# Rotating 96 images by 180 degrees: the first load as two transfers of SyncE, 4 KB and 60 KB of each row, instead of 2 KB by ACT beside 62 KB by SyncE

## The chip, the cores and the metric

The kernel runs on one core of a Trainium2 chip. The metric is the device time of one execution in microseconds. Loads and stores are transfers between the chip's DRAM and the core's on-chip memory, which has 128 partitions. An instruction of SyncE (SP) or ScalarE (ACT) issues a transfer; the core's 16 DMA engines carry it out. Each of the two issuing engines has a queue of its own on all 16 DMA engines: q1 in the profile is SyncE's, q10 is ACT's. A packet here is one contiguous piece of one row.

## What is computed

The input x is float32 of shape 32 x 3 x 256 x 256, 25.17 MB. The output is each 256 x 256 image turned by 180 degrees:

```python
def reference(x):
    return np.rot90(x, k=2, axes=(-2, -1)).astype(np.float32)
```

A flat image of 65,536 elements turned by 180 degrees is the same list of elements in reverse order. There is no arithmetic; all bytes are read once and written once.

## The kernel before

The 96 images are cut into three groups of 32. In a group, each image lies over four partitions, a quarter (E = 16,384 elements, 64 KB) in each, so that a group fills a tile of 128 partitions by 64 KB. The three tiles A, Bt and Ct hold the whole input at once, and a small tile T of 128 x 2,048 is used for swapping.

To turn a group, two things happen. The function `inside` reverses the 16,384 elements of each partition in place, on VectorE: it takes a piece of 2,048 elements from the far end, reversed, into T, copies the matching piece of the near end, reversed, over the far end, and T over the near end. That is four rounds of three copies, 12 copies a tile, 36 in all, all on line 52. The first copy of a tile reads only its last 2,048 columns, and the second reads its first 2,048. The function `store` (line 58) then writes the tile out with the four quarters of each image in reverse order.

SyncE issues all transfers but one, in this order: the long part of A's load, Bt, Ct without its last 1,536 columns (`body`), the last 1,536 columns of Ct, a store of A's first 128 columns, the store of the rest of A, the store of Bt, the store of Ct. ACT issues one transfer, the first 512 columns (2 KB of each row) of A's load, line 70; it has no other work. All loads go through `load`, so that they appear under line 55 in the profile, and all stores under line 58.

An issuing engine waits, before a store, until what it stores has been written. SyncE issues in order, so a store that waits keeps all that follow it waiting. Line 79 adds one wait that the data don't need: the large store of A is not issued before `body` has landed. While SyncE waits for that, the DMA engines have the last 1,536 columns of Ct and the small store of A still to carry. Apart from that wait and VectorE's copies, which are kept in program order, the waits are worked out from which tile pieces an instruction reads and writes.

Of the kernel before, what the change touches and what calls it, by code (L numbers as in the profile page):

```python
# [2 lines left out]

os.environ.setdefault("NEURON_RT_ULTRASERVER_MODE", "4")

# [4 lines left out]

@with_exitstack
def kernel(
    ctx: ExitStack,
    tc: tile.TileContext,
    x: bass.AP,
    out: bass.AP,
):

    nc = tc.nc
    P = 128

    B, C, H, W = x.shape
    L = H * W
    G = 32
    E = L // 4
    J = E // 8

    x4 = x.rearrange("b c h w -> (b c) (h w)").rearrange(
        "(g n) (s e) -> g (n s) e", n=G, s=4)
    o4 = out.rearrange("b c h w -> (b c) (h w)").rearrange(
        "(g n) (s e) -> g n s e", n=G, s=4)  # L40

    pool = ctx.enter_context(tc.tile_pool(name="slots", bufs=1))
    A = pool.tile([P, E], x.dtype, tag="A")
    Bt = pool.tile([P, E], x.dtype, tag="B")
    Ct = pool.tile([P, E], x.dtype, tag="C")
    T = pool.tile([P, J], x.dtype, tag="T")

    def back(t, lo, hi):
        return t[:, hi - 1:(lo - 1 if lo else None):-1]

    def copy(dst, src):
        tc.keep_in_program_order(nc.vector.tensor_copy(out=dst, in_=src))  # L52

    def load(t, g, lo, hi, queue=nc.sync):
        return queue.dma_start(out=t[:, lo:hi], in_=x4[g][:, lo:hi])  # L55

    def store(t, g, lo, hi):
        return nc.sync.dma_start(
            out=o4[g][:, ::-1, lo:hi], in_=t[:, lo:hi])

    def inside(t):
        for lo in range(0, E // 2, J):
            hi = E - lo - J
            copy(T[:, :], back(t, hi, hi + J))
            copy(t[:, hi:hi + J], back(t, lo, lo + J))
            copy(t[:, lo:lo + J], T[:, :])

    TAIL = 1536
    HEAD = 512
    load(A, 0, 0, HEAD, nc.scalar)  # L70
    load(A, 0, HEAD, E)
    load(Bt, 1, 0, E)
    body = load(Ct, 2, 0, E - TAIL)
    load(Ct, 2, E - TAIL, E)
    inside(A)
    LEAD = 128
    store(A, 0, 0, LEAD)
    first = store(A, 0, LEAD, E)
    tc.add_manual_dep(
        first.ins, body.ins.name,  # L80
        mybir.DependencyInfo(mybir.DependencyClass.Sync, mybir.DependencyReason.DATA),
        reason="the first store is queued while the last strip is on its way")
    for g, t in ((1, Bt), (2, Ct)):
        inside(t)
        store(t, g, 0, E)

# [1 line left out]
_INS = ['x']  # L89
_OUTS = [((32, 3, 256, 256), 'float32')]  # L90

# [23 lines left out]
```

## Time and profile before

| | |
|---|---|
| median of 3 runs | 121.97 us (121.96 to 122.07) |
| the profiled execution | 121.97 us |
| its span in the trace | 120.2 us |
| VectorE busy | 44.2 us, 36 copies of 1.23 us |
| bytes moved | 25.17 MB read, 25.17 MB written |
| A's long load, issue to landing | 21.9 us |
| A's 2 KB load by ACT, issue to landing | 22.0 us |
| Bt's load, issue to landing | 40.8 us |
| Ct's store, issue to landing | 42.7 us |
| VectorE waits for A, Bt, Ct | 22.6, 4.3, 4.4 us |

The span runs from the first recorded instruction to the last; the rest of the 121.97 us lies around it. A time from issue to landing holds the time that a transfer waits in its queue behind others: Bt's load is issued at 1.18 us and lands when A's and Bt's bytes have both been carried.

### The profile page before, as it was taken

Reading aid. Unit: us, or ns where it says so; the run is one execution under the profiler, and the core shown is the slowest. Engines: PE = TensorE matmul, PEld = TensorE weight load, DVE = VectorE, ACT = ScalarE, POOL = GpSimd, SP = SyncE. Lnnn points to the kernel's source line nnn. Section 1 sums busy time; section 2 is a strip of 40 time slices with the busy share of each in tenths; the row PEclk is TensorE's granted clock in tenths of the full one; section 3 lists DMA queues with packets and bytes.
Section 4 is the critical chain, followed back from the end, with each engine's and each line's share of the span. In section 5 each row is a group of like instructions: output and inputs, shape, how many; then the busy total and the mean of one; then the engine's idle time right before and its main releaser. Section 6 shows DMA issues by size and latency. Waiting matters only on the chain.

```text
span 120.2 us, 97 instructions
## 1 busy us (share of the span) xinstructions
DVE 44.2 (37%) x36; POOL 0.2 (0%) x4
## 2 busy tenths in 40 slices
DVE  0000000499995099999059999500000000000000
POOL 0000000000000000000000000000000000000000
DMA  9888988899889879979499777988898889888990
GB/s 338 349 349 349 698 349 349 360 654 393 349 349 633 382 316 553 395 316 633 178 452 693 346 346 346 693 349 349 349 698 349 349 349 698 349 349 349 654 393 0
DMA packets 1296, 50.33 MB, mean 419 GB/s; under 512 B 144, under 2 KB 272, under 8 KB 528
## 3 DMA queue, kind: packets, MB, share of 16 engines
q1 hardware_dynamic: 1152, 50.07, 97.0%
q10 hardware_dynamic: 144, 0.26, 0.6%
HBM read 25.17 MB, written 25.17 MB: 419 GB/s over the span
## 4 chain that ended last, share of the span: by engine, by line
DMA 34%; DVE 25%; another core or an unknown queue 4%; issue 1%; SPq 0%; DVEq 0%
DMA Bt<-in_x_dram 34%; DVE T L52 8%; DVE Bt L52 8%; DVE Ct L52 8%; SPq L55 0%; DVEq L52 0%
## 5 line engine op out<-in xcount | busy, mean ns | idle before, releaser
L52 DVE COPY T<-A 128x2048 f32<-128x2048 f32 x4 | 4.9, 1226 | 22.7 <-DMA A<-in_x_dram 22.6
L52 DVE COPY T<-Ct 128x2048 f32<-128x2048 f32 x4 | 4.9, 1227 | 4.5 <-DMA Ct<-in_x_dram 4.4
L52 DVE COPY T<-Bt 128x2048 f32<-128x2048 f32 x4 | 4.9, 1226 | 4.4 <-DMA Bt<-in_x_dram 4.3
L52 DVE COPY Bt<-Bt 128x2048 f32<-128x2048 f32 x4 | 4.9, 1227 | 0.1
L52 DVE COPY A<-A 128x2048 f32<-128x2048 f32 x4 | 4.9, 1227 | 0.1
L52 DVE COPY A<-T 128x2048 f32<-128x2048 f32 x4 | 4.9, 1227 | 0.1
L52 DVE COPY Bt<-T 128x2048 f32<-128x2048 f32 x4 | 4.9, 1227 | 0.1
L52 DVE COPY Ct<-T 128x2048 f32<-128x2048 f32 x4 | 4.9, 1227 | 0.1
L52 DVE COPY Ct<-Ct 128x2048 f32<-128x2048 f32 x4 | 4.9, 1227 | 0.1
L100 POOL MEMSET const-bfloat16-1.0<- 128x1 bf16 x1 | 0.1, 101 | 0.0
L100 POOL MEMSET const-uint8-127<- 128x1 uint8 x1 | 0.1, 101 | 0.0
L100 POOL MEMSET const-float32-0.0<- 128x1 f32 x1 | 0.1, 98 | 0.2 <-issue 0.2
L100 POOL MEMSET const-float32-1.0<- 128x1 f32 x1 | 0.1, 98 | 0.0
## 6 DMA issues: line engine op xcount, KB each, us to landing
out_dram<-A SPq DMA_DIRECT2D x1, 8128.0 KB, 21.1
A<-in_x_dram SPq DMA_DIRECT2D x1, 7936.0 KB, 21.9
Ct<-in_x_dram SPq DMA_DIRECT2D x1, 7424.0 KB, 57.9
Ct<-in_x_dram SPq DMA_DIRECT2D x1, 768.0 KB, 59.3
A<-in_x_dram ACTq DMA_DIRECT2D x1, 256.0 KB, 22.0
out_dram<-A SPq DMA_DIRECT2D x1, 64.0 KB, 35.2
Bt<-in_x_dram SPq DMA_DIRECT2D x1, 40.8
out_dram<-Bt SPq DMA_DIRECT2D x1, 39.8
```

Source lines behind the costliest of these rows:

```text
L52: tc.keep_in_program_order(nc.vector.tensor_copy(out=dst, in_=src))
L100: nc = _bacc.Bacc("TRN2", target_bir_lowering=False, num_devices=1)
```

## The change

The function `load` loses its choice of queue; the first 1,024 columns of A (4 KB of each row) are now loaded by SyncE ahead of the other 15,360 (60 KB of each row), and ACT issues nothing.

```diff
-    def load(t, g, lo, hi, queue=nc.sync):
-        return queue.dma_start(out=t[:, lo:hi], in_=x4[g][:, lo:hi])
+    def load(t, g, lo, hi):
+        return nc.sync.dma_start(out=t[:, lo:hi], in_=x4[g][:, lo:hi])
...
     TAIL = 1536
-    HEAD = 512
-    load(A, 0, 0, HEAD, nc.scalar)
+    HEAD = 1024
+    load(A, 0, 0, HEAD)
     load(A, 0, HEAD, E)
     load(Bt, 1, 0, E)
     body = load(Ct, 2, 0, E - TAIL)
```

In the built program SyncE's list grows from eight transfers to nine, with the two parts of A first; the instructions of VectorE and GpSimd and their waits are the same.

## The prediction

> **What bounds the kernel now.** I read the page first, then the issue rows, then the waits of the DMA queue's own engine, then a table of stretches. The page:
>
> ```profile
> span 120.2 us, 97 instructions
> DVE 44.2 (37%) x36; POOL 0.2 (0%) x4
> ...
> DMA packets 1296, 50.33 MB, mean 419 GB/s; under 512 B 144, under 2 KB 272, under 8 KB 528
> ## 3 DMA queue, kind: packets, MB, share of 16 engines
> q1 hardware_dynamic: 1152, 50.07, 97.0%
> q10 hardware_dynamic: 144, 0.26, 0.6%
> ```
>
> VectorE works 37% of the span; the 16 DMA engines hold packets for 97.0 + 0.6 = 97.6% of it. q1 is SyncE's queue, q10 is ACT's; 144 packets on q10 are 128 rows of 2 KB and 16 four-byte completion writes. The page's chain of waits gives "DMA Bt" 34% and VectorE 25%, but it follows semaphores, and the store queue hides behind it. The waits of SyncE's queue show the real end:
>
> ```profile
> SPq L111 <- DMA out_dram<-Ct: 38.6, 1, 38.6
> SPq L58 <- DMA Ct<-in_x_dram: 33.1, 2, 32.5
> SPq L58 <- DMA A<-in_x_dram: 20.1, 1, 20.1
> SPq L58 <- DVE Ct L52: 15.2, 1, 15.2
> ```
>
> The last thing awaited is the last store, for 38.6 us, although VectorE was through at 76.7 us. So the time is: start of the transfer stream, plus the stream without a hole, plus the close.
>
> **The stream in numbers.** The packet records of the trace give one size, one duration: 512 B 27 ns, 2,048 B 84 ns, 6,144 B 234 ns, 59,392 B 2,192 ns, 63,488 B 2,342 ns, 65,024 B 2,399 ns, 65,536 B 2,418 ns. Each DMA engine carries 8 rows of every transfer, so one engine's work is 8 x (84 + 2,342 + 2,418 + 2,192 + 234 + 27 + 2,399 + 2 x 2,418) = 8 x 14,532 ns = 116.26 us. The start of the span:
>
> ```profile
> 0.73 0.38 ACTq L55 DMA_DIRECT2D A<-in_x_dram  x1
> 0.73 0.39 SPq L55 DMA_DIRECT2D A<-in_x_dram  x1
> 1.18 0.42 SPq L55 DMA_DIRECT2D Bt<-in_x_dram  x1
> 1.63 1.01 SPq L55 DMA_DIRECT2D Ct<-in_x_dram  x2
> ```
> ```profile
> 0.00:1.00 1.00, 0.00 (x0) 0.20 (x4) 1.00 0.00 0
> 1.00:2.00 1.00, 0.00 (x0) 0.00 (x0) 1.00 2.70 889
> 2.00:3.00 1.00, 0.00 (x0) 0.00 (x0) 1.00 0.34 127
> 3.00:4.00 1.00, 0.00 (x0) 0.00 (x0) 1.00 0.00 0
> 4.00:5.00 1.00, 0.00 (x0) 0.00 (x0) 1.00 1.22 528
> ```
>
> The first are start and duration of the issues. In the second the last two columns are DMA share and GB/s, booked to the stretch in which a packet starts: 889 GB/s in 1 us is 14 packets of 63,488 B, 127 is two more, and no further packet starts before 4 us. In the packet records the first of the 16 starts at 1.755 us, 1.02 us after the issue, fifteen by 2.08 and the sixteenth at 2.82. The fifteen take 2.89 to 3.30 us where later packets of the size take 2.34: an excess of 0.55 to 0.95 us, which I call the cold excess. All sixteen end at 4.78 to 5.22; less 2.342 that is as if data ran from 2.44 to 2.88 us on. ACT's packets, issued in the same instant as SyncE's, start only when the first long packet of their engine is over (4.78 us and on), and then the two queues alternate: a 2 KB row, a long row, a 2 KB row.
>
> Check of the sum: 2.88 + 116.26 = 119.14; the last data packet ends at 119.05. The last landing is at 119.39, and the span ends at 120.18. The profiled execution took 121.97 us, so 1.79 lies around the span, and it equals the median of the runs, 121.97; I work with its numbers as they are.
>
> **The change, part by part.**
>
> *ACT's issue goes.* One instruction of 0.38 us beside SyncE's of 0.39; ACT has no other work. Gain 0 on the path.
>
> *SyncE issues one more transfer, ahead of the others.* Its issues stand 0.45 us apart (0.73, 1.18, 1.63). So the 4 KB rows are issued at 0.73, the 60 KB rows at 1.18, Bt at 1.63 in place of 1.18, Ct's two from 2.08. Bt's packets are wanted when A's are through, at about 21.8 us, so 20 us hide the shift. Were there no such cover, 0.45 us would be paid.
>
> *The bytes.* Each engine has 8 packets of 4,096 B and 8 of 61,440 B for 8 of 2,048 and 8 of 63,488. Midway between the 2,048 B and 6,144 B rows is 159 ns, midway between 59,392 B and 63,488 B 2,267 ns. 8 x (159 + 2,267) = 19.41 us; before 8 x (84 + 2,342) = 19.41 us. Difference 0.
>
> *The hand-over from the first transfer to the second.* This is new: the engines now run dry unless the 60 KB packets are there when the 4 KB packets are through. The short ones last 8 x 0.159 = 1.27 us from when data runs, so to 2.44 + 1.27 = 3.71 us on the earliest engine. The second transfer, issued at 1.18, has packets at 1.18 + 1.02 = 2.20 if it goes as the first of them did, and 1.18 + 2.09 = 3.27 if as the latest. Margin 0.44 us at the worst. With no cold excess the short ones would be through at 1.755 + 1.27 = 3.03, and the latest engine would idle 0.24 us, which the vanished excess of 0.55 more than pays. So 0.
>
> *The cold excess with short packets* is in no row. Ends: it vanishes (-0.95 us, the largest excess), or it is paid again for the second transfer (+0.95); paid for each of 8 short packets (8 x 0.65 = +5 us) is excluded by the nearest rows: at 59 us the 6,144 B loads, also eight short packets in a row per engine at the same place of each row, keep 234 ns with one exception of 291, and 512 B stores keep 27 ns. These are warm, but they show that eight short reads in a row run without a gap. I take 0 change: the excess is once per engine at its first read, whatever the packet's length.
>
> *VectorE.* Its first copy reads the end of A's rows, so it waits for the long transfer alone (before: landed 22.59, ACT's part 22.76). In the new order the long rows are last on each engine, so it starts about 0.17 us later. Copies of A end at about 37.8 + 0.2; Bt lands at 41.96. Over 4 us hide it. The small store at 26.39 moves with it and is not wanted before 60.6 us.
>
> *The join of loads and stores.* The large store of A waits for Ct's long part (landed 59.56, issued 59.63, first packets 60.84) while 8 x (234 + 27) = 2.09 us of short packets cover it. Nothing of it changes but the engines' relative lag, now 0.44 us from first to last; the last engine has over 0.6 us of cover left (2.09 less landing and issue, 1.4 to 1.5), and it sets the end.
>
> Sum: 0, so **121.97 us**, give or take 0.2: half of the 0.44 us by which engines differ in their start, since the engine that ends last may be another.
>
> A rule that would make another sum. The two issues above stand side by side at 0.73, each as long as one alone (0.38 and 0.39, against 0.42 for Bt's). The Trainium skill (Perfetto Trace Analysis, "DMA Instruction — HWDGE (DVE, Sync)") says that the block which makes descriptors is shared by the two issuing engines and locked by one at a time, and counts the wait for the lock as part of the instruction; by it one of the two should last about 0.77 us, and if SyncE's descriptors stood behind ACT's, dropping ACT's would bring the stream forward by up to 0.38 us, to 121.59. The durations show no such wait, so the sum goes without it.
>
> **The rivals.**
>
> *Slower: the cold start is paid twice.* With long first packets, one read of 2.3 us covers everything that happens behind it. A short first transfer takes that cover away: if the 60 KB packets need not 2.09 but over 2.5 us from their issue at 1.18 (that is, are usable only after 3.7 us), the engines stand idle. From there it decides. For it: one of sixteen engines began 0.74 us after the other fifteen, and I see no transfer that starts behind an emptying queue at that point. Price: from nothing up to the excess once more, 0.95 us; the middle, with 0.55, gives 122.5; span of the case 122.2 to 122.9.
>
> *Faster: the cold excess comes from the two queues filling at once, or from sixteen long reads starting in step.* For it: the one engine that started late, at 2.82, took 2.349 us, no excess. Against it: that engine ended at 5.17, with the others, so it may only have been recorded late. Price: up to the whole excess, 121.0; likelier about half, 121.5; span 121.0 to 121.75.
>
> *The change does nothing that it says:* the program does have the two transfers first on SyncE and none on ACT, so this leaves only that all stays within the trace's scatter, which is the forecast.
>
> **How the numbers follow.** Forecast 0.57, slower rival 0.29, faster rival 0.14. A measurement of this kernel can tell about 0.2%, 0.24 us, from no change; the forecast's own range, 121.77 to 122.17, lies inside. The range for 8 in 10 takes the forecast whole, the slower rival up to 122.65 (about 0.2 of its 0.29) and the faster one down to 121.55 (about 0.06 of 0.14): 0.83. Faster 0.14, within 0.57, slower 0.29.
>
> **What would show it.** In the new trace: the first packet near 1.76 us; 4 KB packets of 159 ns after a first one with about 0.7 us more; the 60 KB packets starting from 3.7 to 4.2 us with no hole before them and 2,267 ns each, the first ones too. All packets of A end on the last engine near 22.15 us as before, VectorE starts at about 22.8. A hole between 4 KB and 60 KB packets, or long first 60 KB packets, is the slower rival; 60 KB packets from 3.1 to 3.5 us the faster one. I am wrong altogether if time is lost later than 5 us, for instance a hole at 60 to 62 us from a greater lag between engines.

## The result and the profile after

The changed kernel takes 122.41 us (median of 6 runs, 122.15 to 122.60) against 122.01 us (121.96 to 122.07) of the kernel before in the same comparison: ratio 1.003, 95% interval 1.0016 to 1.0043. It is slower, by about 0.4 us. Run again later beside other kernels it took 122.56 against 122.04, ratio 1.0038 (1.0025 to 1.0052). The profiled execution, 122.19 us, is one of the two quickest of its six, 0.22 us above the profiled one of before. A ratio here is the one that has an interval; it is not exactly the quotient of the two medians.

The page of the changed kernel, the lines that answer to those of before:

```profile
span 120.4 us, 97 instructions
...
DVE 44.2 (37%) x36; POOL 0.2 (0%) x4
...
DMA packets 1296, 50.33 MB, mean 418 GB/s; under 512 B 144, under 2 KB 272, under 8 KB 528
## 3 DMA queue, kind: packets, MB, share of 16 engines
q1 hardware_dynamic: 1296, 50.33, 97.5%
```

Nothing new is to be carried: the same 1,296 packets and 50.33 MB, now all on SyncE's queue, and packets for 97.5% of the span as before. The waits of SyncE's queue:

```profile
SPq L111 <- DMA out_dram<-Ct: 38.5, 1, 38.5
SPq L58 <- DMA Ct<-in_x_dram: 33.1, 2, 32.5
SPq L58 <- DVE A L52: 21.9, 1, 21.9
...
SPq L58 <- DMA A<-in_x_dram: 1.4, 1, 1.4
```

The end is the same wait for the last store. The 20.1 us that SyncE waited for ACT's part of A have become 1.4 us, because the short transfer now lands first; SyncE then waits for VectorE's first three copies instead, so the small store is issued at 26.69 us where it was 26.39. The start, as issues and as stretches (the last two columns are DMA share and GB/s by packets that start in the stretch):

```profile
0.73 0.86 SPq L55 DMA_DIRECT2D A<-in_x_dram  x2
1.64 0.43 SPq L55 DMA_DIRECT2D Bt<-in_x_dram  x1
2.11 1.21 SPq L55 DMA_DIRECT2D Ct<-in_x_dram  x2
```
```profile
1.00:2.00 1.00, 0.00 (x0) 0.00 (x0) 1.00 0.51 57
2.00:3.00 1.00, 0.00 (x0) 0.00 (x0) 1.00 0.63 143
3.00:4.00 1.00, 0.00 (x0) 0.00 (x0) 1.00 2.34 983
4.00:5.00 1.00, 0.00 (x0) 0.00 (x0) 1.00 0.75 324
```

57 + 143 = 200 KB are 49 packets of 4,096 B begun before 3 us, of 128. Sixteen engines that began at 1.755 us and took 159 ns a packet would be through with all 128 by 3.03 us. So the cold phase is there with short packets too. The packet records show its shape: 95 of the 128 short packets take 159 ns; the other 33 all start before 3.1 us, and on most engines one of the first two takes 0.4 to 1.15 us. The issue rows (KB, us from issue to landing) show how late the slowest engine is:

```profile
A<-in_x_dram SPq DMA_DIRECT2D x1, 7680.0 KB, 21.7
...
A<-in_x_dram SPq DMA_DIRECT2D x1, 512.0 KB, 4.0
out_dram<-A SPq DMA_DIRECT2D x1, 64.0 KB, 35.2
```

The 512 KB transfer, issued at 0.73 us, has landed whole at 4.75. Its sixteen completions, one from each DMA engine, lie between 3.93 and 4.75 us, 0.82 us apart.

To compare kernels whose first packets differ in size, I use one number for each DMA engine: the end of its first long packet of A, less the normal duration of all that it has carried until then. For a kernel whose short part comes last or by ACT that is one long packet; for one that has it first, eight short ones and a long one. I call it the engine's **data start**; for the kernel before it is the 2.44 to 2.88 us of the prediction.

| | mean of 16 engines | slowest engine |
|---|---|---|
| before | 2.62 | 2.88 |
| changed | 2.65 | 3.12 |
| changed, run again | 2.75 | 3.31 |

The excess of a packet is what it takes beyond the normal duration of its size. The mean hardly moves in the first pair: the excess in packets begun before 6 us is 0.695 us per engine before and 0.688 after; in the second execution it is 0.794. The slowest engine is 0.24 us later, and in the second execution 0.43. That is most of the loss, which is 0.22 us in the first profile and 0.59 in the second (122.56 against 121.97 us).

### The profile page after: what moved, and what is told of

It reads as the page before. It is cut to its first block, busy times and chain, and to the rows that moved or that the text cites. A ratio compares the mean times of both kernels' runs of the same rounds, so it can differ in the third digit from the quotient of the medians.

```text
span 120.4 us, 97 instructions
## 1 busy us (share of the span) xinstructions
DVE 44.2 (37%) x36; POOL 0.2 (0%) x4
## 2 busy tenths in 40 slices
DMA packets 1296, 50.33 MB, mean 418 GB/s; under 512 B 144, under 2 KB 272, under 8 KB 528
## 3 DMA queue, kind: packets, MB, share of 16 engines
q1 hardware_dynamic: 1296, 50.33, 97.5%
## 4 chain that ended last, share of the span: by engine, by line
DMA 34%; DVE 25%; another core or an unknown queue 4%; issue 1%; SPq 1%; DVEq 0%
DMA Bt<-in_x_dram 34%; DVE T L52 8%; DVE Bt L52 8%; DVE Ct L52 8%; SPq L55 1%; DVEq L52 0%
```

## How the slowest engine's lag reaches the end

A lag made at the start could be made good later. In the changed kernel it is not. The small store of A is the last short thing in the queue behind the loads, so its landing on the slowest engine marks the end of loading. In 17 of the 18 profiled executions of this study the time less that landing is 60.30 to 60.46 us (in the 1 KB form 60.65); for before it is 121.97 - 61.62 = 60.35, for the changed kernel 122.19 - 61.89 = 60.30, for its repetition 122.56 - 62.18 = 60.38. Whatever the loads lose is settled by 62 us, and it is paid in full; the 1 KB form lost 0.3 us more behind that point.

The engines that are ahead lose part of their lead at the join. Before, then after, in stretches, and the issue of the large store of A (start and duration):

```profile
59.00:60.00 1.00, 0.00 (x0) 0.00 (x0) 1.00 1.05 436
60.00:61.00 1.00, 0.00 (x0) 0.00 (x0) 1.00 2.06 851
61.00:62.00 1.00, 0.45 (x1) 0.00 (x0) 1.00 1.26 538
```
```profile
59.63 0.55 SPq L58 DMA_DIRECT2D out_dram<-A  x1
```
```profile
59.00:60.00 1.00, 0.00 (x0) 0.00 (x0) 1.00 0.97 406
60.00:61.00 1.00, 0.00 (x0) 0.00 (x0) 1.00 0.93 371
61.00:62.00 1.00, 0.18 (x1) 0.00 (x0) 1.00 2.55 1073
```
```profile
59.86 0.55 SPq L58 DMA_DIRECT2D out_dram<-A  x1
```

Before, eight long packets of the large store (65,024 B) start in 60 to 61 us, the first at 60.84. After, none does: the first starts at 61.06, because SyncE may not issue the large store until the slowest engine has landed Ct's long part (59.78 us, for 59.55 before). The first engines then have a short hole: in the packet records the earliest engine is through with the small store at 60.86 us, 0.20 us before the first packet of the large store. The slowest engine has no hole: its last short packet ends at 61.45, and its first large-store packet starts at 61.45. The spread of landings shrinks from 0.59 us (small store) to 0.33 (large store of A). The hole is not all of that, since it shrinks before as well, from 0.42 to 0.29, with no engine idle there.

## The experiments

Each was timed beside the kernel before, in five rounds; medians in us. "Slowest" is the data start of the slowest engine in the profile of that run, which is one execution and not the median one.

| kernel | first load, in order of issue | median | before beside it | ratio (95% interval) | slowest |
|---|---|---|---|---|---|
| before | 2 KB by ACT, 62 KB by SyncE | | | | 2.88 |
| changed, again | 4 KB, 60 KB by SyncE | 122.56 | 122.04 | 1.0038 (1.0025 to 1.0052) | 3.31 |
| sp1k | 1 KB, 63 KB by SyncE | 122.52 | 122.03 | 1.0033 (1.0019 to 1.0047) | 3.31 |
| sp2k | 2 KB, 62 KB by SyncE | 122.11 | 121.98 | 1.0021 (1.0008 to 1.0033) | 2.91 |
| sp8k | 8 KB, 56 KB by SyncE | 121.96 | 122.04 | 0.9998 (0.9985 to 1.0011) | 2.63 |
| sp8k, again | the same | 121.92 | 122.06 | 0.9988 (0.9977 to 1.0000) | 2.70 |
| sp16k | 16 KB, 48 KB by SyncE | 121.94 | 122.04 | 0.9994 (0.9981 to 1.0008) | 2.67 |
| one64k | 64 KB by SyncE | 122.15 | 121.98 | 1.0015 (1.0004 to 1.0025) | 3.06 |
| long_first | 60 KB, 4 KB by SyncE | 122.09 | 121.98 | 1.0017 (1.0006 to 1.0027) | 2.75 |
| act4k | 4 KB by ACT, 60 KB by SyncE | 122.08 | 121.98 | 1.0009 (1.0001 to 1.0018) | 2.96 |
| act8k | 8 KB by ACT, 56 KB by SyncE | 122.10 | 122.06 | 1.0008 (0.9996 to 1.0019) | 2.96 |
| swap4k | 4 KB by SyncE, 60 KB by ACT | 122.29 | 122.06 | 1.0012 (1.0002 to 1.0023) | 3.27 |
| split60 | 4 KB, 28 KB, 32 KB by SyncE | 122.44 | 122.06 | 1.0031 (1.0019 to 1.0042) | 3.09 |
| pitch4k | 4 KB pieces 4 KB apart, 60 KB | 122.05 | 122.04 | 1.0007 (0.9998 to 1.0016) | 2.61 |
| pitch68k | 4 KB pieces 68 KB apart, 60 KB | 122.35 | 122.03 | 1.0017 (1.0006 to 1.0027) | 2.88 |
| region64k | 4 KB pieces 64 KB apart, 8 MB on | 122.38 | 122.03 | 1.0033 (1.0019 to 1.0048) | 2.90 |
| tail12k | as changed, Ct's tail 12 KB | 123.29 | 122.03 | 1.0099 (1.0076 to 1.0122) | 3.14 |

The last column does not order the profiled times by itself. From the slowest data start to the last landing of Bt it is 39.01 to 39.12 us in ten of the eighteen profiles, but 39.31 in region64k's, 39.37 in long_first's, 39.41 in sp16k's and 39.44 in pitch4k's. The profiles of pitch4k (122.16 us) and sp16k (122.23) are therefore slower than that of before (121.97), although their slowest engines start 0.27 and 0.21 us earlier. So an excess on later packets of A and Bt is a second term, and only the median times show pitch4k and sp16k level with before.

**Is it the queue or the order?** My first theory (L) was that short packets which come first on idle engines spread them; the rivals were that ACT's queue is missed (Q), or that the long packets come late behind the short ones (H). Four kernels, as edits of the changed one.

The size of before on the queue of after:
```diff
-    HEAD = 1024
+    HEAD = 512
```

> The first load comes as 2 KB and 62 KB of each row, both by SyncE, the short part first: the queue of the changed kernel with the size of the one before. Theory L (short packets that come first on idle engines spread the engines further apart at the start, and the last one sets the time): slower than before by 0.2 to 0.6 us, 122.2 to 122.6. Theory Q (it is ACT's queue that is missed): also slower, 122.2 to 122.6. Theory H (the long packets come late behind the short ones): the cover is only 0.67 us, so 122.8 or more, with a hole before the 62 KB packets.

The size of after on the queue of before:
```diff
-    load(A, 0, 0, HEAD)
+    load(A, 0, 0, HEAD, nc.scalar)
```

> 4 KB of each row by ACT beside 60 KB by SyncE: the size of the changed kernel, the queue of the one before. Theory L: the first packet on each engine is a long one, so as before, 121.9 to 122.1, start spread about 0.44 us. Theory Q: also 121.9 to 122.1. Size alone as the cause would give 122.2 to 122.6.

No split:
```diff
-    load(A, 0, 0, HEAD)
-    load(A, 0, HEAD, E)
+    load(A, 0, 0, E)
```

> The first load is one transfer of 64 KB of each row by SyncE, nothing by ACT. Theory L: the first packets are long, so 121.9 to 122.1. Theory Q: ACT's queue is missing, so 122.2 to 122.6 as in the changed kernel. Theory H: no short packets to run out of, 121.9 to 122.1.

The other order:
```diff
-    load(A, 0, 0, HEAD)
     load(A, 0, HEAD, E)
+    load(A, 0, 0, HEAD)
```

> The two transfers of the changed kernel, both by SyncE, in the other order: 60 KB of each row first, then the 4 KB. Theory L: long packets first, so 121.9 to 122.1 with a start spread of about 0.44 us. Theory Q: ACT's queue is missing, so 122.2 to 122.6.

No theory comes out whole. All four lie between 122.08 and 122.15, with ratios of 1.0009 to 1.0021, above the kernel before and below the changed one's 1.003, though all four intervals reach into that of the changed kernel (1.0016 to 1.0043). H falls: 2 KB first did not cost 0.8 us, and there is no hole before its 62 KB packets. Q in its plain form falls too, since one64k and long_first lose only half as much as it needs; that they lose at all leaves it a part for the moment. L expected more of sp2k (122.2 at least) and less of one64k (122.1 at most); the times of act4k and long_first came as it expected. The size alone (act4k) is not it. Either 4 KB first by SyncE is a case of its own, or the 122.41 was partly chance.

**Is it this size?** The changed kernel unaltered, and larger short parts (the edits change HEAD to 2048 and 4096).

> The changed kernel itself, unaltered, beside the other three on one chip. If its loss is its own, 122.3 to 122.5 again, with the slowest engine's 4 KB landing 0.7 us or more behind the first. If the difference to the 2 KB form (122.11) was chance between runs, 122.1.

> 8 KB and 56 KB of each row, both by SyncE, short part first. Theory L (short packets on idle engines spread the engines apart): the cold phase of 1 us ends within three packets of 0.31 us, so a spread between the 4 KB form's and that of a long first packet, 122.1 to 122.3. If the loss grows with the bytes that are read at the same place of all rows: more than with 4 KB, 122.5 to 122.8.

> 16 KB and 48 KB of each row, both by SyncE, short part first. Theory L: a first packet of 0.61 us nearly covers the cold phase, so like one load of 64 KB, 122.1 to 122.2. If the loss grows with the bytes at the same place of all rows: 122.6 or more.

The loss came back, 122.56. With 8 KB and 16 KB first it is gone: 121.96 and 121.94. Both have nothing on ACT's queue, so Q falls for good: the queue isn't needed. That the loss grows with the bytes at one place of all rows falls as well. L had expected too much of both, 122.1 to 122.3 and 122.1 to 122.2. The start of the 8 KB form, in stretches, and its row among the issues:

```profile
1.00:2.00 1.00, 0.00 (x0) 0.00 (x0) 1.00 0.66 106
2.00:3.00 1.00, 0.00 (x0) 0.00 (x0) 1.00 0.58 213
3.00:4.00 1.00, 0.00 (x0) 0.00 (x0) 1.00 1.01 426
4.00:5.00 1.00, 0.00 (x0) 0.00 (x0) 1.00 2.44 1049
```
```profile
A<-in_x_dram SPq DMA_DIRECT2D x1, 1024.0 KB, 4.7
```

In the two microseconds before 3 us 319 KB are begun where the changed kernel begins 200. The transfer has landed whole at 0.73 + 4.7 = 5.4 us, and its sixteen completions lie 0.45 us apart, not 0.82.

**A smaller one.** HEAD at 256:

> 1 KB and 63 KB of each row, both by SyncE, the short part first: the short packets last 8 x 0.046 = 0.37 us. If the lag grows with the number of bytes read at one place: smaller than with 2 KB (122.11), 122.0 to 122.1. If any short first packet spreads the engines: 122.3 to 122.6. If the long packets come too late behind so short a cover: a hole before them, 122.3 or more.

122.52: a short first part does spread the engines, and the loss is not in step with its bytes. Its start in half microseconds:

```profile
2.00:2.50 0.50, 0.00 (x0) 0.00 (x0) 1.00 5.24 1741
2.50:3.00 0.50, 0.00 (x0) 0.00 (x0) 1.00 1.17 387
3.00:3.50 0.50, 0.00 (x0) 0.00 (x0) 1.00 0.30 129
```

129 GB/s in half a microsecond is 64.5 KB, one packet, recorded from 3.27 us, where all short ones had ended by 2.54. That looks like H, but this packet takes 2.41 us, with hardly any excess, and is through at 5.68; the slowest engine is another, whose long packet starts at 2.70 and takes 3.37 (6.06). With packets of 46 ns the short ones are over before the cold excess has been paid, and the long ones pay it: 15 of 16 take 2.87 to 3.37 for a normal 2.38.

**Where the pieces lie.** Three kernels that differ from the changed one in the 4 KB pieces alone.

```diff
-    load(A, 0, 0, HEAD)
+    flat = x.rearrange("b c h w -> (b c h w)").rearrange("(p e) -> p e", e=HEAD)
+    nc.sync.dma_start(out=A[:, 0:HEAD], in_=flat[0:P, :])
```

> As the changed kernel, but the 4 KB pieces of the first transfer are read from one run of 512 KB (piece p from 4 KB times p), not from 128 rows 64 KB apart; A's first 1,024 columns so hold other data. If the cold spread comes from all engines reading the same place of rows 64 KB apart: spread of the 4 KB landings down from 0.8 to below 0.4 us, cold excess below 0.5 us, 121.9 to 122.1. If it comes from short packets on idle engines whatever they read: as the changed kernel, spread 0.8 us, 122.3 to 122.5.

```diff
-    load(A, 0, 0, HEAD)
+    flat = x.rearrange("b c h w -> (b c h w)")[0:P * (E + HEAD)].rearrange(
+        "(p e) -> p e", e=E + HEAD)
+    nc.sync.dma_start(out=A[:, 0:HEAD], in_=flat[:, 0:HEAD])
```

> As the changed kernel, but the 4 KB pieces of the first transfer are read 68 KB apart in place of 64 KB, over the same 8 MB; A's first 1,024 columns so hold other data. If the spread of the changed kernel comes from all rows being read at the same place of a 64 KB step: as with pieces 4 KB apart, spread of the 4 KB landings 0.3 to 0.5 us, 121.9 to 122.1. If only a compact run of 512 KB helps: spread 0.8 us, 122.3 to 122.6.

```diff
-    load(A, 0, 0, HEAD)
+    nc.sync.dma_start(out=A[:, 0:HEAD], in_=x4[1][:, 0:HEAD])
```

> The control to the two kernels that read other data: the 4 KB pieces come from the rows of the second group, 64 KB apart as in the changed kernel, but 8 MB further on, so that the long pieces don't follow them in memory. If the 64 KB step is the cause: as the changed kernel, spread 0.7 to 0.9 us, 122.3 to 122.6. If reading other bytes than the long transfer's own rows is what helped: 121.9 to 122.1.

The rows of the 512 KB transfer among the issues, in that order (4 KB apart, 68 KB apart, 64 KB apart in other rows):

```profile
A<-in_x_dram SPq DMA_DIRECT2D x1, 512.0 KB, 3.4
```
```profile
A<-in_x_dram SPq DMA_DIRECT2D x1, 512.0 KB, 3.8
```
```profile
A<-in_x_dram SPq DMA_DIRECT2D x1, 512.0 KB, 3.8
```

The compact run, the first of the three, lands 0.6 us earlier than the changed kernel's (3.4 for 4.0), its completions lie 0.36 us apart in place of 0.82, and the time is that of before, 122.05; its excess before 6 us is 0.546 us per engine, where I had expected less than 0.5. In stretches:

```profile
1.00:2.00 1.00, 0.00 (x0) 0.00 (x0) 1.00 0.43 53
2.00:3.00 1.00, 0.00 (x0) 0.00 (x0) 1.00 0.80 279
```

332 KB are begun before 3 us, against 200. Pieces in other rows, 64 KB apart, are as slow as the changed kernel (122.38, ratio 1.0033; 164 KB begun), although their one profile has a spread of 0.52 where I had expected 0.7 at least. So reading other bytes is not the cure. Pieces 68 KB apart lie between: their median is 122.35, with 254 KB begun and completions 0.75 us apart, but their interval, 1.0006 to 1.0027, reaches into those of both the others. So it is not settled whether the 64 KB step matters. The compact run differs from the slow form in two ways, the step of 4 KB and the small region of 512 KB, and the runs do not part these. Nor did the two controls lose their time at the start in their profiles: the slowest data starts are 2.88 and 2.90, as before, and the 0.14 and 0.33 us that these executions (122.11 and 122.30) took beyond before's came later; in region64k's an excess of 0.213 us per engine lies between 6 and 22 us. The Trainium skill (DMA: Bandwidth & Descriptors, "Latency and other measured facts") gives copy rates for row pitches of large powers of two, from 512 KiB to 8 MiB, and says that 4 KiB more per row brought a pitch of 4 MiB back to the full rate. The 64 KB of this case lies below its list; here 4 KB more is not shown to restore the time (122.35 at 68 KB, 122.38 at 64 KB).

**The join.** The edit sets TAIL to 3072, so that more cover stands between Ct's long part and the large store.

> The changed kernel with Ct's last 3,072 columns in the second transfer in place of 1,536, which gives the join of loads and stores 2.1 us more cover (eight packets of 6 KB more per engine). If the loss is made by engines that stand idle at the join: it goes, 122.0 to 122.1. If the slowest engine's lag, made at the start, sets the end: no change, 122.3 to 122.6, though the other engines no longer wait.

123.29, far from both expectations: the larger tail has a price of its own (and the cover that it adds is 8 x (460 - 234) ns = 1.8 us, less than the 2.1 us of the expectation). Its row among the issues and the stretches:

```profile
Ct<-in_x_dram SPq DMA_DIRECT2D x1, 1536.0 KB, 60.0
```
```profile
59.00:60.00 1.00, 0.00 (x0) 0.00 (x0) 1.00 0.88 307
60.00:61.00 1.00, 0.00 (x0) 0.00 (x0) 1.00 0.94 394
61.00:62.00 1.00, 0.00 (x0) 0.00 (x0) 1.00 2.70 1135
62.00:63.00 1.00, 0.30 (x1) 0.00 (x0) 1.00 0.16 69
```

Of the 128 twelve-kilobyte packets, normally 460 ns, 42 take longer, up to 1,074; the rate falls to 307 GB/s in 59 to 60 us. One engine is left behind: its first large-store packet is the 69 GB/s of 62 to 63 us, while the other fifteen start theirs in the stretch before. As a trial of the join it is inconclusive, but it holds one fact: no engine waits at the join now, the spread of 1.28 us at the small store is still 1.23 at the last landing, and the time less the small store's landing is still 123.20 - 62.81 = 60.39. So here too the slowest engine sets the end, though the others did not wait.

**Can the two terms be parted?** In the changed kernel the long packets of A between 6 and 13.5 us also show an excess, 0.142 us per engine, where before has 0.000. I wanted to know whether that is a part of the loss, and whether one short packet on an idle engine is enough to spread them. Two more forms were timed beside these, act8k and the 8 KB form again.

```diff
     load(A, 0, 0, HEAD)
-    load(A, 0, HEAD, E)
+    load(A, 0, HEAD, E // 2)
+    load(A, 0, E // 2, E)
```

> The changed kernel with its 60 KB transfer cut in two, 28 KB and 32 KB of each row, so that no 60 KB rows are read; eight more packets per engine cost 8 x 8 ns = 0.07 us. If the 60 KB rows' excess from 6 to 13 us is a term of the loss: that excess below 0.05 us and 122.2 to 122.3. If the start alone makes the loss: 122.4 to 122.6 as the changed kernel.

```diff
-    load(A, 0, 0, HEAD)
-    load(A, 0, HEAD, E)
+    load(A, 0, 0, HEAD)
+    load(A, 0, HEAD, E, nc.scalar)
```

> 4 KB of each row by SyncE beside 60 KB by ACT, the changed kernel's sizes on exchanged queues. A 4 KB packet may come first on an engine, but a long one follows at once. If eight short packets in a row on idle engines are what spreads them: 121.9 to 122.1, spread of A's landing below 0.6 us. If one short packet first is enough, or the sizes alone count: 122.3 to 122.6.

> 8 KB of each row by ACT beside 56 KB by SyncE. Its first packets are long ones, so about as the kernel before, 121.9 to 122.1.

> The 8 KB and 56 KB form by SyncE again. If it is level with the kernel before: 121.9 to 122.1. If its profile (121.77, all engines 0.2 us earlier) is what it mostly does: 121.8 and below the kernel before by over 0.1%.

split60 lost as much as the changed kernel, 122.44, but its excess from 6 to 22 us was 0.116, not below 0.05, so it did not part the two terms: the length of 60 KB is not what makes that excess, and my expectation missed. Nor are the rows themselves: act4k and swap4k read the same 60 KB rows on the two queues with an excess of 0.000 and 0.001, and long_first reads them by SyncE with 0.227. All eight profiles in which SyncE alone loads A and one part is 4 KB show it, 0.116 to 0.272; the four with two queues have 0.001 at most. The traces of the changed kernel say that little of it is on the path: from the slowest engine's data start to the last landing of Bt it is 41.96 - 2.88 = 39.08 us before, 42.24 - 3.12 = 39.12 after and 42.50 - 3.31 = 39.19 in the repetition, so the excess fell mostly on engines that were ahead, and 0.04 and 0.11 us of it on the slowest.

swap4k did not do what it was meant to: 32 short packets, two an engine on average, are begun by 3.3 us and the next only at 5.03; the first sixteen 60 KB packets start from 2.65 to 3.59 us. In its profile the slowest data start, counted with two short packets, is 3.27, and the small store's landings lie 0.79 us apart, as in the repetition of the changed kernel (3.31 and 0.78). So in this one execution two short packets spread the engines as eight do; its ratio, 1.0012, lies between the two answers. act8k is level, 1.0008. The 8 KB form on SyncE is level once and 0.12% below before once, the interval touching 1.0000; over both comparisons I call it level with the kernel before and better than the changed kernel, and no version is shown to beat both.

## Why the prediction was wrong

**What bounds the kernel: right.** The transfer stream is full, the last store ends it, and VectorE, which started 0.29 us later (22.91 for 22.62), cost nothing.

**Issues, bytes: right.** The first packet starts at 1.753 us (1.755), the 4 KB packets mostly take 159 ns and the 60 KB packets 2,267, as interpolated; 33 of the 60 KB packets between 6 and 13.5 us take longer, which the sum did not have (0.04 us on the slowest engine, 0.11 in the repetition). With ACT's issue gone the stream does not come forward: the first packet stands 1.02 us behind the issue in both, so the gain of up to 0.38 us which the prediction estimated by the rule of the Trainium skill (Perfetto Trace Analysis, "DMA Instruction — HWDGE (DVE, Sync)") is not there.

**Hand-over: right.** The sixteen 60 KB packets that come first start from 3.61 to 4.40 us, each within some tens of nanoseconds of the end of a short one, and they pay no second excess. So the slower rival, "the cold start is paid twice", whose figure of 122.5 the result is near, is not what happened; that it came near is luck.

**The cold excess with short packets: this step failed.** I wrote: "I take 0 change: the excess is once per engine at its first read, whatever the packet's length". The mean bears that out in the first pair, 0.695 and 0.688 us (0.794 in the repetition), though it lies on 33 short packets, about two an engine. But the time is set by the slowest engine, and I gave its start "half of the 0.44 us by which engines differ" as a symmetric 0.2. What the runs showed in its place: with 4 KB pieces first the slowest engine's data start goes from 2.88 to 3.12, 3.31, 3.09 (split60) and 3.14 us (tail12k), later in each of these four, while 8 KB or 16 KB pieces bring it to 2.63 to 2.70. So the term that the sum had at 0 measured 0.24 us in the first profile and 0.43 in the second. The nearest rows that I used, short packets in a row on busy engines, spoke of warm engines and could not show it.

**The join:** I named a hole at 60 to 62 us from a greater lag as a sign of being wrong altogether. It is there on the early engines, 0.20 us, but as an effect of the lag: the slowest engine has no hole.

**What is shown and what is open.** Shown: the changed kernel's loss is made in the loads, by 62 us, and for the most part (0.24 of 0.27 us at the small store's landing in the first profile, 0.43 of 0.56 in the second) by the slowest engine's start. By the median times it is there with pieces of 4 KB (and 1 KB) read first by SyncE from rows 64 KB apart, and it is gone with pieces of 8 or 16 KB and with a compact run of 4 KB pieces. Not shown: that the start decides in every form. region64k's profile lost 0.33 us with hardly any lag at the start, and pitch4k's and sp16k's started early and lost it again. Whether 2 KB costs less than 4 KB is not parted by the intervals. Open: why short pieces on idle engines delay single engines so unevenly, why 8 KB cost nothing, and what makes the excess between 6 and 22 us. The changed kernel and the 8 KB form have two profiles, every other form one. Runs of the changed kernel differ by 0.45 us among themselves, those of before by 0.11 in the same comparison and by up to 0.64 in the longer ones, so a single profile says little about a form; I do not give a mechanism.

## What to carry to other kernels

In a transfer-bound kernel with sixteen engines in parallel, work out the loads for the slowest engine and not for the mean: what it had lost by the end of the loads was paid at the end of the kernel, to 0.16 us, in 17 of 18 profiles. Here a first transfer of 4 KB pieces from rows 64 KB apart made that engine later and cost 0.3 to 0.4%; pieces of 8 KB or 16 KB did not. Rows measured on busy engines say nothing about the first read of idle ones, and a cost that is bounded only by such rows should get a range on the slow side.

## What the runs showed of the hardware, not expected

- A packet's duration on warm engines is not always fixed by its size: of the 128 pieces of 6 KB at 59 us all but a few kept 234 ns (eight took 235 to 291 before, two 239 and 248 after), while 42 of the 128 pieces of 12 KB at the same point took over 460 ns, up to 1,074, in all 0.44 us more per engine.
- Two transfers issued in the same instant on SyncE's and ACT's queues did not start together. In the kernel before every engine took SyncE's first long packet and then went back and forth between the queues, packet by packet, and ACT's 2 KB rows began only at 4.78 us; in swap4k ACT's first 60 KB packet starts at 2.65 us, SyncE's first 4 KB packet at 1.75.
- In 17 of 18 executions with quite different starts, the time from the slowest landing of the small store to the end kept within 0.16 us (60.30 to 60.46).
